# A hybrid encoder block on one core: the head in channel layout, a reordered SSM, and one gate chunk moved ahead of attention

## Chip, cores and metric

The kernel runs on one core of a Trainium2 chip. The metric is the device time of one execution in microseconds. All inputs are fp32, and a matmul operand is cut into two fp32r parts, a high part (a cast) and a low part (what the cast lost), so that one product costs three matmuls: high by high, high by low and low by high.

## What is computed

A block of 16 meta tokens and 1024 tokens (L = 1040) with 1024 channels passes through an RMSNorm, two mixers in parallel, a gated merge, an output projection, and then a convolutional FFN. Cut to what matters here:

```python
xn = rmsnorm(h, norm_mix_g)
q, k, v, f_logit, u, gates = split(xn @ w_in)
y_a = forgetting_attention(q, k, v, f_logit, b_forget) @ w_attn_out   # 8 heads of 64
z = gelu(s5(u, ...))                    # complex diagonal SSM, 32 groups of 16 channels, 64 states
zg = z @ w_glu
y_s = zg[..., :1024] * sigmoid(zg[..., 1024:])
g = sigmoid(gates)                      # 2048 wide
merged = g[..., :1024] * y_a + g[..., 1024:] * y_s
h = h + merged @ w_o
h = h + conv_ffn(rmsnorm(h, norm_ffn_g))
out = rmsnorm(h, norm_final_g)[16:]     # meta tokens dropped
```

## The kernel before

The program is written in one order, and a planner that simulates the run draws from it the order of instructions on each engine; on the chip each engine then keeps that order. `after(a, b)` pins `a` behind `b` on their engine without a semaphore. Tiles come from pools with a tag and a number of buffers; a tile waits until the last user of the buffer that it gets is done. Tags are shared between quite different tiles, so that, say, an x tile can sit in the place of an SSM table ("Gm", "Tm", "Wi", "sy", "tq").

**Head.** The normalised input is wanted with channels on partitions, as `xhi` and `xlo` [128, 8, 1040], for every projection from it. The first block of 272 tokens comes from the host already transposed (`x0t`): ScalarE casts it times g1 (L350), VectorE cuts the low part (L353), and the u product (`part`, L327 to L329) runs on features without the norm; the factor of each token, spread over the partitions through a transpose (L370), is multiplied in afterwards (L377). The other 768 tokens are loaded in rows, 128 a tile: a square with a running sum on ScalarE, a power on GpSimd, a multiply on VectorE (L340), eight transposes on TensorE (L191), a cast on ScalarE (L193) and a cut on VectorE (L129), and then the u product of their block (96 matmuls of 256 columns). Block 0's own normalised features are made last. u goes to memory (`u_d`) in 32 small stores and comes back grouped for the SSM.

**SSM.** `ssm` has three parts: small steps on VectorE on [128, 32] tiles, from the step sizes to the powers of lambda; a rotation table for either half of the groups; then for each quarter `tables(qt)`, with the output tables Gm and Tm (Tm through eight small transfers) and after them the input table Wi, and `chain(qt)`: U times Wi on TensorE, a rotation, two scans, a rotation back into the state St, and then Y = Gm St + Tm U, GELU, a store to `y_d`. The small steps may begin behind the features of tile 4.

**Gates.** `gate_chunk` makes 128 of the 2048 gate channels: 72 matmuls of 342 columns in three groups, each followed by a sigmoid and a store into `g_d`. The upper eight chunks are written after the SSM and fill TensorE beside it. Their weights come over GpSimd's queue and are cut by a cast and an accumulating transfer. The first chunk's weight (`gate0`) waits for the last features. The lower eight are spread between attention's steps, `GA = [2, 1, 1, 3]` for the four pairs of heads (the eighth follows attention), with a tanh in place of the sigmoid.

**Then** come `load_z` (32 small loads and the cuts of z and its sums), `forget_w` (the forget gate's weight), the first pair's q and k projection, `forget` (the forget gate, its log-sigmoid and running sum) and GLU in a seven-product block form.

Of the kernel before, what the change touches and what calls it, by code (L numbers as in the profile page):

```python
# [50 lines left out]
def block_kernel(ctx, tc, x, meta, g1, x0t, g1t, w_q, w_k, w_v, w_f, w_u, w_g, b_f, w_ao, lam_d, bw_d, cw_d,  # L51
# [118 lines left out]
    def norm_factor(pl, src, n, bufs=10, sq=None):  # L170
# [3 lines left out]
        S.activation(sq[:n], src, AF.Square, accum_out=ss[:n])  # L174
        va = pl.tile([P, 1], F, tag="vr", name="vr", bufs=3)
        V.tensor_scalar(va[:n], ss[:n], 1.0 / D, EPS, ALU.mult, ALU.add)
        rs = pl.tile([P, 1], F, tag="rs", name="rs", bufs=bufs)
        GP.tensor_tensor(rs[:n], va[:n], nhalf[:n], ALU.pow)
        return rs
# [107 lines left out]
    xa = [sp.tile([P, 4, UN], F, tag="tq", name="xa", bufs=3) for _ in range(2)]  # L287
    g1T = n1.tile([P, KD], F, name="g1T")
    S.dma_start(g1T, g1t)
    S.dma_start(xm, meta)  # L290
# [12 lines left out]
    xts = [sp.tile([P, D], F, tag=tag, name="xt", bufs=n) for tag, n in (("Wi", 2), ("Gm", 2), ("sy", 3)) for _ in range(n)]  # L303
    g1B = xts.pop(4)
    g1_load = S.dma_start(g1B, g1.partition_broadcast(P))

    place = dict(zip((3, 4, 1, 2, 5, 6), xts))
    place[0] = xm

    def load_x(i):  # L310
        load(place[i], x[P * (i - 1):P * i])

    for i in range(1, 7):
# [20 lines left out]
    def factors(i):  # L334
        n = TILES[i][1]
        return norm_factor(n1, place[i][:n], n)

    def features(i, rs, behind=None):
        t, n = TILES[i]
        xn = V.scalar_tensor_tensor(out=place[i][:n], in0=place[i][:n], scalar=rs[:n], in1=g1B[:n],  # L340
                                    op0=ALU.mult, op1=ALU.mult)
        if behind is not None:
            after(xn, behind)
        return to_feature(place[i], n, xhi, xlo, t)[-1]

    first = [mm_ps() for _ in range(4)]
    for j in range(4):
        for k in (2 * j, 2 * j + 1):
            src, hi = xa[j // 2][:, k % 4], xhi[:, k, :UN]
            cp_ = S.activation(hi, src, AF.Copy, scale=g1T[:, k:k + 1])  # L350
            if k == 1:
                after(g1_load, cp_)
            V.scalar_tensor_tensor(out=xlo[:, k, :UN], in0=src, scalar=g1T[:, k:k + 1], in1=hi.bitcast(F),  # L353
                                   op0=ALU.mult, op1=ALU.subtract)
        S.copy(uh[j], uraw[j])
        split_lo(V, ul[j], uraw[j], uh[j])
        for m in range(4):
            for k in (2 * j, 2 * j + 1):
                part(first[m], m, k, 0, UN)
    for i in (7, 8):  # L360
        place[i] = sp.tile([P, D], F, tag="Tm", name="xt", bufs=2)
        load_x(i)

    rs0 = [factors(i) for i in range(3)]
    tp = t_ps()
    for i, rs in enumerate(rs0):
        t, n = TILES[i]
        rb = sp.tile([P, P], F, tag="wi", name="rb", bufs=2)
        V.tensor_copy(rb[:n], rs[:n].broadcast_to([n, P]))
        PE.transpose(tp[:, t:t + n], rb[:n], ident[:n, :n])  # L370
    rsB = sp.tile([P, UN], F, tag="wr", name="rsB", bufs=2)
    S.copy(rsB, tp[:, :UN])
    for i in (3, 4):
        ready = features(i, factors(i))
    n_log = len(ssm_log)
    for m in range(4):
        V.tensor_tensor(us[m][:, :, :UN // CH], by_chunks(first[m][:, :UN]), by_chunks(rsB), ALU.mult)  # L377

    for b, (t, n) in enumerate(UBLK[1:]):
        if b:  # L380
            for i in (3 + 2 * b, 4 + 2 * b):
                last = features(i, factors(i))
        for m in range(4):
            ps = mm_ps()
            for k in range(KD):
                part(ps, m, k, t, n)
            S.copy(us[m][:, :, t // CH:(t + n) // CH], by_chunks(ps[:, :n]))
        if b == 2:
            for i in range(3):
                features(i, rs0[i], last)  # L390
# [4 lines left out]
    gate0 = [sp.tile([P, KD, P], dt, tag=tag, name="g0", bufs=n)  # L395
             for dt, tag, n in ((F, "Wi", 2), (R, "sy", 3), (R, "Wi", 2))]
    late.append(last)
    after(GP.dma_start(gate0[0], w_g[KD]), last)
    S.copy(gate0[1], gate0[0])
    lo_by_dma(gate0[2], gate0[1], w_g[KD])  # L400

# [4 lines left out]
    ssm_tables, ssm_chain = next(ssm_steps)  # L406
# [4 lines left out]
    def begin(q):  # L411
        ssm_tables(q)
# [3 lines left out]
    begin(0)  # L416
    begin(1)
    for q in range(4):
        run(chains[q])
# [5 lines left out]

    st_g = ExitStack()
    gp_ = pool(st_g, "gates", side="right")

    okeep = {}

    def gate_chunk(i, pl, tanh):
# [3 lines left out]
        for t, n in QBLK:  # L435
# [5 lines left out]
            else:  # L441
                gs = pl.tile([P, LQ // 3], F, tag="gs", name="gs", bufs=2)
                S.activation(gs, ps[:, :n], AF.Sigmoid)
                S.dma_start(g_d[P * i:P * i + P, t:t + n], gs)
# [7 lines left out]
    for i in range(KD, 2 * KD):  # L452
# [3 lines left out]
    st_f = ExitStack()  # L456
    fp = pool(st_f, "fgate", side="right")
    fraw = fp.tile([P, KD, H], F, name="fraw")
# [1378 lines left out]
```

## Time and profile before

| | us |
|---|---|
| three runs | 1481.59, 1489.31, 1491.31 |
| median of the runs | 1489.31 |
| span of the profiled execution | 1485.7 |
| TensorE busy in it | 1440.4 (97%) |
| VectorE, ScalarE, GpSimd busy | 1071.4, 712.2, 742.1 |

The profiled execution is one more execution; its own time is its span, from the first to the last instruction, and it lies inside the range of the three runs. PE is TensorE's matmuls and PEld its weight loads, DVE is VectorE, ACT ScalarE, POOL GpSimd, SP the engine that only issues transfers; L12 is line 12 of the kernel before. A matmul's own duration overlaps with the next one's, so that the pace is read from a stretch of time and a count and not from the mean of one; some matmul records can be missing. The granted clock is 1.00 where TensorE runs at full speed.

### The profile page before, as it was taken

What the parts mean: (1) busy time and instruction counts of PE and PEld (TensorE: products, weight loads), DVE (VectorE), ACT (ScalarE), POOL (GpSimd) and SP (SyncE); (2) the same over time, 40 slices, a digit from 0 to 9 for tenths busy, and PEclk for the clock granted to TensorE, in tenths of its full rate; (3) what the DMA queues carried; (4) which work ended last, traced back from release to release, by engine and by line L of the source; (5) the groups of instructions that cost most, each with busy time, mean ns of one, the idle gap of its engine ahead of it and who ended that gap; (6) DMA issues with size and microseconds to landing.
All of it is one profiled execution on the core that took longest, in us unless ns stands there. A gap on an engine that the chain in (4) does not pass through costs nothing. (4 is left out here: it accounts for less than half of the span.)

```text
span 1485.7 us, 26584 instructions
## 1 busy us (share of the span) xinstructions
PE 1440.4 (97%) x9712; PEld 1358.8 (91%) x9712; DVE 1071.4 (72%) x2173; ACT 712.2 (48%) x1384; POOL 742.1 (50%) x850
## 2 busy tenths in 40 slices
PE   7999997999999999999999999999999999998997
PEld 7989996998899999999888999999999999777886
DVE  6879648881566676647468987888877776788785
ACT  6434675541555665543546534444444445543433
POOL 1311125752456465524863144455544426789766
PEclk9999999999999999999999999999999999999999
DMA  6366571551127342047885135676653215765513
GB/s 246 86 157 157 128 163 50 177 160 43 48 79 178 93 111 90 26 148 256 257 158 185 57 109 141 178 199 188 174 143 100 84 57 180 286 203 148 168 40 114
DMA packets 91032, 206.72 MB, mean 139 GB/s; under 512 B 14651, under 2 KB 25531, under 8 KB 90517
## 3 DMA queue, kind: packets, MB, share of 16 engines
q1 hardware_dynamic: 69380, 159.73, 32.9%
q0 software_dynamic: 15296, 34.63, 13.2%
q10 hardware_dynamic: 6224, 10.65, 1.9%
q8 instruction: 77, 1.26, 0.3%
q14 instruction: 55, 0.44, 0.1%
HBM read 165.90 MB, written 69.35 MB: 158 GB/s over the span
## 5 line engine op out<-in xcount | busy, mean ns | idle before, releaser
L159 PE MATMUL mm<-xhi,whi 128*128 128x342 f32 (+2 forms) x488 | 159.4, 327 | 1.0 <-DVE q L129 1.0
L161 PE MATMUL mm<-xhi,wlo 128*128 128x342 f32 (+2 forms) x488 | 158.3, 325 | 0.0
L160 PE MATMUL mm<-xlo,whi 128*128 128x342 f32 (+2 forms) x488 | 157.7, 324 | 0.0
L1079 POOL TENSOR_TENSOR ov<-ov,og 128x1024 f32<-128x1024 f32 x21 | 51.1, 2434 | 125.6 <-ACT og L1078 121.7
L129 DVE TENSOR_TENSOR sw<-sf,sw 128x512 fp32r<-128x512 f32 x72 | 66.6, 925 | 50.0 <-ACT sw L1070 49.8
L1070 ACT CAST sw<-sf 128x512 fp32r<-128x512 f32 x72 | 44.9, 624 | 106.2 <-POOL sf L1196 74.5
L159 PEld LDWEIGHTS mm<-xhi,whi 128*128 128x128 f32 x488 | 91.9, 188 | 2.1 <-PE sp L714 0.8
L161 PEld LDWEIGHTS mm<-xhi,wlo 128*128 128x128 f32 x488 | 91.8, 188 | 0.3
L160 PEld LDWEIGHTS mm<-xlo,whi 128*128 128x128 f32 x488 | 91.9, 188 | 0.2
L763 ACT CAST th<-tp 128x256 fp32r<-128x256 f32 (+3 forms) x120 | 56.2, 472 | 62.5 <-PE tp L756 30.1
L129 DVE TENSOR_TENSOR tl<-tp,th 128x256 fp32r<-128x256 f32 (+3 forms) x120 | 65.2, 547 | 25.1 <-ACT th L763 23.7
L1196 POOL TENSOR_TENSOR sf<-raw,sf 128x512 f32<-128x512 f32 x36 | 59.1, 1641 | 44.8 <-DVE sw L129 44.7
L1196 POOL TENSOR_TENSOR sf<-raw 128x512 f32<-128x512 f32 x36 | 48.0, 1332 | 66.9 <-DMA raw<-in_w_up_dram 35.9
L221 PE MATMUL mm<-xhi,sw 128*128 128x258 f32 (+1 forms) x288 | 81.0, 281 | 0.0
L219 PE MATMUL mm<-xhi,sw 128*128 128x258 f32 (+1 forms) x288 | 80.8, 281 | 0.0
L220 PE MATMUL mm<-xlo,sw 128*128 128x258 f32 (+1 forms) x288 | 80.7, 280 | 0.0
L728 POOL TENSOR_SCALAR pt<-pt,nm 128x144 f32<-128x144 f32 (+4 forms) x72 | 51.8, 731 | 48.5 <-DVE nm L727 47.5
L1248 DVE SCALAR_TENSOR_TENSOR ov<-hv,cwt,ov 128x1024 f32<-128x1024 f32 x36 | 72.5, 2014 | 0.1
L1070 ACT CAST sw<-raw 128x512 fp32r<-128x512 f32 x70 | 43.0, 621 | 53.3 <-PE sp L221 25.5
L726 ACT ACTIVATE pt<-pt,nm 128x144 f32<-128x144 f32 (+4 forms) x72 | 52.9, 735 | 26.1 <-DVE nm L725 25.7
L719 DVE CUSTOM_DVE_ANT_0 pt<-sp,fb 128x328 f32<-128x328 f32 (+8 forms) x112 | 46.4, 430 | 20.0 <-PE sp L714 11.1
L756 PE MATMUL tp<-ident,pt 128*128 128x128 f32 (+1 forms) x360 | 58.3, 270 | 0.1
(708 smaller groups left out, 5702.1 us busy)
## 6 DMA issues: line engine op xcount, KB each, us to landing
raw<-in_w_up_dram SPq DMA_DIRECT2D x44, 512.0 KB, 3.6
t_d<-in_w_dn_dram POOLq DMA_DIRECT2D x44, 256.0 KB, 7.0
ar<-a_d SPq DMA_DIRECT2D x44, 256.0 KB, 5.1
wr<-t_d SPq DMA_DIRECT2D x44, 256.0 KB, 2.8
a_d<-ov SPq DMA_DIRECT2D x21, 512.0 KB, 2.6
wr<-in_w_dn_dram SPq DMA_DIRECT2D x33, 256.0 KB, 3.8
t_d<-in_w_dn_dram SPq DMA_DIRECT2D x22, 256.0 KB, 4.2
t_d<-t_d SPq DMA_DIRECT2D x22, 256.0 KB, 4.7
```

The source lines that it names most:

```text
L129: return eng.tensor_tensor(out_, src, hi.bitcast(F), ALU.subtract)
L159: yield PE.matmul(ps, whi[:, i, :], ahi[:, i], start=(i == 0), stop=False)
L160: yield PE.matmul(ps, whi[:, i, :], alo[:, i], start=False, stop=False)
L161: yield PE.matmul(ps, wlo[:, i, :], ahi[:, i], start=False, stop=(i == k - 1))
L219: PE.matmul(ps, a[0][:, i], bh, start=(i == 0 and not joins), stop=False, skip_group_check=True)
L220: PE.matmul(ps, a[0][:, i], bl, start=False, stop=False, skip_group_check=True)
L221: PE.matmul(ps, a[1][:, i], bh, start=False, stop=(i == kh - 1), skip_group_check=True)
L756: PE.transpose(tp[:kn, o:o + n], p_[:n, k0:k0 + kn], ident[:n, :n])
L763: S.copy(th[:kn, z:tw], tp[:kn, z:tw])
L1070: S.copy(hi, src)
L1196: sums.append(GP.tensor_tensor(f_, a, b, op))
L1248: V.scalar_tensor_tensor(out=o, in0=h_[:, j:SEQ + j], scalar=cwc(j, m), in1=o, op0=ALU.mult, op1=ALU.add)
```

## The change

- All 1040 tokens come transposed from the host (`xbt` for blocks 1 to 3), beside the row tiles that still give the factors. Blocks 0 and 1 go through the u product without the norm, and their u is multiplied by the factors later; blocks 2 and 3 are multiplied by the spread factors first. At the end blocks 0 and 1 get their normalised features in place. No x tile is transposed on the chip; the factors of all nine tiles are spread by a transpose.
- The first pieces of x and w_u are one channel block wide. meta, the step sizes and lambda come over GpSimd's queue; the broadcast of g1 is gone.
- The small steps may begin behind block 1's first features. The first gate chunk's weight is loaded without waiting for the last features, and the other gate weights wait for block 3's.
- `tables` is split into `input_tables` and `output_tables`. A quarter's input table and its U product come first; the output tables come after that quarter's state (for quarter 0 ahead of quarter 1's start). `dt8` is copied on ScalarE, and the second rotation is made in chain 2.
- y and the upper gate chunks go to memory over GpSimd's queue. Every second one of the eight loads of the last quarter of z goes there too.
- The forget gate's weight is made before the gate chunks and the gate itself straight after them, ahead of z and of the q/k projection.
- One chunk of the lower eight is made with the upper ones (`AHEAD = 1`), and attention's first pair has one less.

The diff, cut to its core:

```diff
-    for j in range(4):
-        load(xa[j // 2][:, 2 * (j % 2):2 * (j % 2) + 2], x0t[:, 2 * j:2 * j + 2])
-        load(uraw[j], w_u[:, 2 * j:2 * j + 2])
...
+    FIRST = [(0, 1), (1, 1), (2, 2), (4, 2), (6, 2)]
+    for k, n in FIRST:
+        load(xT[0][k // 4][:, k % 4:k % 4 + n], x0t[:, k:k + n])
+        load(uraw[k // 2][:, k % 2:k % 2 + n], w_u[:, k:k + n])
+
+    def load_block(b, tag):
+        xT[b] = [sp.tile([P, 4, UBLK[b][1]], F, tag=tag, name="xT", bufs=2) for _ in range(2)]
+        for h_ in range(2):
+            load(xT[b][h_], xbt[b - 1, :, 4 * h_:4 * h_ + 4])
...
+    load_block(1, "Wi")
+    for i in range(5, 9):
         load_x(i)
...
+    def factors(b):
+        tp = t_ps()
+        t0, n_ = UBLK[b]
+        for i in TB[b]:
+            t, n = TILES[i]
+            rs = norm_factor(n1, place[i][:n], n, behind=head[0])
+            rb = rbs[:n, i % 3]
+            V.tensor_copy(rb, rs[:n].broadcast_to([n, P]))
+            PE.transpose(tp[:, t - t0:t - t0 + n], rb, ident[:n, :n])
+        S.copy(spread[b], tp[:, :n_])
+
+    def features(b, k):
+        t, n = UBLK[b]
+        src, hi = xT[b][k // 4][:, k % 4], xhi[:, k, t:t + n]
+        cp_ = S.activation(hi, src, AF.Copy, scale=g1T[:, k:k + 1])
+        cut = V.scalar_tensor_tensor(out=xlo[:, k, t:t + n], in0=src, scalar=g1T[:, k:k + 1], in1=hi.bitcast(F),
+                                     op0=ALU.mult, op1=ALU.subtract)
+        return cp_, cut
+
+    def normed_features(b):
+        t, n = UBLK[b]
+        for q in range(2):
+            V.tensor_tensor(xT[b][q], xT[b][q], spread[b].unsqueeze(1).broadcast_to([P, 4, n]), ALU.mult)
+        return [features(b, k)[1] for k in range(KD)][-1]
...
+    load_block(2, "Tm")
+    load_block(3, "Gm")
+    for i in range(1, 5):
         load_x(i)
...
+    for b in (2, 3):
+        last = normed_features(b)
+        if b == 2:
+            gate0 = [sp.tile([P, KD, P], dt, tag=tag, name="g0", bufs=n)
+                     for dt, tag, n in ((F, "Tm", 2), (R, "sy", 3), (R, "Tm", 2))]
+            GP.dma_start(gate0[0], w_g[KD])
...
+        if b == 3:
+            for q in (0, 1):
+                factors(q)
+            for q in (0, 1):
+                normed_features(q)
         for m in range(4):
...
     def begin(q):
-        ssm_tables(q)
+        ssm_in(q)
         chains[q] = ssm_chain(q)
         next(chains[q])
 
     begin(0)
+    ssm_out(0)
     begin(1)
     for q in range(4):
+        next(chains[q])
+        if q:
+            ssm_out(q)
         run(chains[q])
...
-                S.dma_start(g_d[P * i:P * i + P, t:t + n], gs)
+                GP.dma_start(g_d[P * i:P * i + P, t:t + n], gs)
...
-    for i in range(KD, 2 * KD):
+    for i in [*range(KD, 2 * KD), *range(AHEAD)]:
         run(gate_chunk(i, gp_, False))
...
+    forget()
...
-                SY.dma_start(zt[GC * g:GC * g + GC], ym[g])
+                (GP if m == 3 and g % 2 else SY).dma_start(zt[GC * g:GC * g + GC], ym[g])
...
-    forget_w()
     qk = qk_tiles(0)
     run(project_qk(0, qk))
-    forget()
...
-    GA = [2, 1, 1, 3]
+    GA = [1, 1, 1, 3]
...
-            dt8 = big("dt8", [P, HQ, NCH])
-            V.tensor_copy(dt8, dec[:, qt * HQ:qt * HQ + HQ].unsqueeze(2).broadcast_to([P, HQ, NCH]))
...
+            S.copy(dt8, dec[:, qt * HQ:qt * HQ + HQ].unsqueeze(2).broadcast_to([P, HQ, NCH]))
+            GP.memset(dt8[:, :, 0:1], 0.0)
+            if qt == 2:
+                rot.append(rotation(1))
...
-            S.dma_start(y_d[qt], Y)
+            GP.dma_start(y_d[qt], Y)
```

More of the change, by code (lines that the diff above doesn't have):

```diff
@@ L347, in block_kernel @@
[L347 to L356, printed above, removed]
+    head = []
@@ new lines, in u_product, with us_part @@
+    def u_product(b, m):
+        ps = mm_ps()
+        for k in range(KD):
+            part(ps, m, k, *UBLK[b])
+        return ps
+    def us_part(b, m):
+        t, n = UBLK[b]
+        return us[m][:, :, t // CH:(t + n) // CH]
+    first = [mm_ps() for _ in range(4)]
+    for k0, n in FIRST:
+        j, sl = k0 // 2, slice(k0 % 2, k0 % 2 + n)
+        for k in range(k0, k0 + n):
+            features(0, k)
+        cp_ = S.copy(uh[j][:, sl], uraw[j][:, sl])
+        split_lo(V, ul[j][:, sl], uraw[j][:, sl], uh[j][:, sl])
@@ L357, in block_kernel @@
         for m in range(4):
[L358 removed]
+            for k in range(k0, k0 + n):
                 part(first[m], m, k, 0, UN)
[L360 to L361 removed]
+    head.append(cp_)
+    load_block(2, "Tm")
+    load_block(3, "Gm")
+    for i in range(1, 5):
         load_x(i)
[L364 to L374, printed above, removed]
+    for m in range(4):
+        S.copy(us_part(0, m), by_chunks(first[m][:, :UN]))
+    for k in range(KD):
+        ready = features(1, k)[1]
     n_log = len(ssm_log)
+    for b in (2, 3):
+        factors(b)
     for m in range(4):
[L377 to L382, printed above, removed]
-        for m in range(4):
[L384 to L390, printed above, removed]
+        ps = u_product(1, m)
+        S.copy(us_part(1, m), by_chunks(ps[:, :UBLK[1][1]]))
```

157 lines of the change are left out of this document (80 added, 77 removed).

## The prediction

> **What bounds the kernel now.** I read the page first, then the windows view cut at the points where the first 260 us change character, then TensorE's waits there.
>
> ```profile
> span 1485.7 us, 26584 instructions
> ...
> PE 1440.4 (97%) x9712; PEld 1358.8 (91%) x9712; DVE 1071.4 (72%) x2173; ACT 712.2 (48%) x1384; POOL 742.1 (50%) x850
> ```
>
> TensorE is busy for 97% of the span, so an edit can win only where TensorE stands idle, runs at a reduced clock, or has work taken from it. The windows view says where. Its columns are the busy time of each engine (instructions in brackets), then granted clock, DMA share and rate.
>
> ```profile
> core 0: us, PE busy (x) PEld busy (x) DVE busy (x) ACT busy (x) POOL busy (x), PEclk, DMA share, GB/s
> 0.00:7.30 7.30, 0.00 (x0) 0.00 (x0) 1.33 (x11) 3.30 (x5) 1.05 (x8) 1.00 0.71 198
> 7.30:23.00 15.70, 15.68 (x107) 15.35 (x107) 10.26 (x20) 12.01 (x21) 2.75 (x5) 1.00 1.03 412
> 23.00:26.20 3.20, 0.08 (x1) 0.00 (x0) 3.20 (x7) 3.17 (x7) 0.00 (x0) 0.88 0.92 365
> 26.20:33.00 6.80, 6.79 (x34) 6.57 (x35) 6.80 (x14) 4.07 (x8) 2.65 (x4) 0.55 0.03 9
> 33.00:73.50 40.50, 38.09 (x320) 37.04 (x319) 32.93 (x142) 15.12 (x30) 12.61 (x31) 1.00 0.30 75
> 73.50:98.00 24.50, 21.75 (x136) 20.86 (x137) 16.95 (x41) 7.28 (x15) 7.18 (x16) 0.93 0.89 214
> 98.00:195.20 97.20, 97.20 (x690) 95.37 (x688) 78.05 (x135) 52.25 (x90) 11.73 (x18) 1.00 0.56 136
> 195.20:224.80 29.60, 29.55 (x187) 29.23 (x185) 15.62 (x20) 22.62 (x33) 7.88 (x4) 1.00 0.65 141
> 224.80:238.00 13.20, 10.38 (x49) 8.66 (x49) 13.03 (x14) 7.01 (x17) 8.94 (x8) 0.74 0.15 41
> 238.00:257.00 19.00, 13.65 (x103) 12.40 (x102) 13.88 (x25) 11.05 (x21) 9.85 (x9) 1.00 0.11 30
> ...
> 390.00:455.00 65.00, 63.48 (x445) 61.79 (x446) 40.53 (x164) 36.06 (x84) 35.19 (x67) 1.00 0.18 57
> 455.00:640.00 185.00, 184.36 (x1288) 180.00 (x1287) 124.22 (x550) 108.82 (x265) 108.62 (x219) 1.00 0.39 104
> ```
>
> The head (u projection) runs to 73.5, SSM beside gate chunks to 195, the q/k projection to 225, the forget gate to 238, then GLU. Up to 257 TensorE is idle for 23.7 us by these rows: 7.3, 3.1, 2.4, 2.75, 2.8 and 5.35 us. Behind three of the gaps the clock is short: 0.55 over 6.8 us loses 3.05 us, 0.93 over 24.5 us loses 1.7, 0.74 over 13.2 us loses 3.4, of which I put some 0.8 inside the gap itself, so 2.6. The gaps have these causes:
>
> ```profile
> PE mm L327 <- ACT uh L355: 7.3, 1, 7.3
> PE sp L191 <- DVE vr L176: 3.1, 1, 3.1
> PE mm L518 <- POOL wf L129: 2.9, 1, 2.9
> PE sp L1730 <- ACT Wi L1714: 2.7, 1, 2.7
> ...
> PE sp L191 <- DVE xlo L129: 1.7, 1, 1.7
> ```
>
> They are the first weight cast, the transposes that wait for a normalised tile (twice), the forget weight, and SSM's input matrix, released late. The change touches every one of them. By the page "TensorE: Matmul & The Clock Gate" of the Trainium skill (part 1, the clock gate) the clock halves after an idle window of about 3.4 us, which would leave these gaps of 2.7 to 3.2 us unpunished and take 7 us off what the change can win; the rows with 0.55, 0.93 and 0.74 behind such gaps disagree, so that reading gets no weight here.
>
> **The change part by part.** *Head, TensorE.* Tokens of blocks 1 to 3 now arrive with channels on partitions, so the transposes of L191 go; nine transposes of a broadcast factor (three before) stay. A block of 96 matmuls keeps its pace:
>
> ```profile
> 44.00:55.44 11.44, 11.44 (x99) 11.44 (x98) 11.29 (x68) 2.16 (x6) 3.95 (x16) 1.00 0.00 0
> 124.00:134.10 10.10, 10.10 (x66) 9.93 (x65) 10.03 (x19) 7.06 (x9) 2.48 (x4) 1.00 0.69 200
> ```
>
> The first w_u piece holds one channel block instead of two, so the cast in front of the first matmul does half the elements and its transfer half the bytes: 7.3 becomes about 6.0 us. Block 0 keeps the 14.6 us from 7.3 to 21.9 that it has now, then three blocks of 11.44 us and about 1 us for the six added small transposes end at 6.0 + 14.6 + 34.3 + 1.0 = 55.9, against 73.5 now: 17.6 us at best. The pieces are the 3.1 and 2.4 us of gaps, 3.05 of clock, 1.3 at the start and some 7 of transposes. I keep 4 us for new waits of the same kind, since the factor transposes still sit in TensorE's order behind ACT's square and POOL's power: the gates start at 60, and the head wins 13.5 us (bounds 5, where one gap with its clock loss comes back and the gates wait for normalised blocks, and 17.6).
>
> *Head, DMA.* 768 tokens by 1024 channels, 3.1 MB of transposed x, are added and the 0.5 MB broadcast of g1 goes: at the 412 GB/s of the second row 6.4 us more traffic. x0t, w_u and block 1 are 4.3 MB, 10.3 us at that rate, so block 1 is there by 14 us and needed at 20.6; blocks 2 and 3, behind four x tiles, end at 8.5 MB, by 25 us, or by 30 with the waits for the tiles whose place they take, and are needed at 32 and 43.5. Cost on the path: 0. Without that cover each late 1 MB block would stop TensorE for 2.5 us.
>
> *Head, DVE and ACT.* These rows price the cut into high and low parts:
>
> ```profile
> L340 DVE SCALAR_TENSOR_TENSOR xt<-xt,rs 128x1024 f32<-128x1024 f32 x8 | 10.1, 1276 | 0.7 <-POOL rs L178 0.7
> L129 DVE TENSOR_TENSOR xlo<-tp,xhi 128x512 fp32r<-128x512 f32 x6 | 4.2, 698 | 0.0
> L353 DVE SCALAR_TENSOR_TENSOR xlo<-xa,g1T,xhi 128x272 fp32r<-128x272 f32 x8 | 3.6, 498 | 4.6 <-ACT xhi L350 4.6
> L350 ACT ACTIVATE xhi<-xa,g1T 128x272 fp32r<-128x272 f32 x8 | 3.7, 512 | 1.1 <-DMA xa<-in_x0t_dram 1.0
> ```
>
> Now two tiles cost DVE 2 x 1.28 + 4 x 0.69 = 5.3 us. A new block costs two 1024-wide multiplies at the 1.28 of L340 and eight cuts at no more than 0.5: 6.5 us. Over four blocks that is 4.8 us more, plus 4.0 for cutting block 1 a first time, so about 9 us more DVE work; ACT gets eight 0.51 us casts a block. DVE is busy for 54.5 of the first 73.5 us, so this fits before 73.5; but if the gates are to start at 56 it fills DVE completely, which is my second reason for the 4 us. So the SSM's small steps, though allowed earlier (behind block 1's cut, not behind tile 4), get their turn only in part earlier.
>
> *SSM.* Input tables and U's product go ahead of the output tables, dt8's copy goes to ACT, the second rotation moves behind chain 2's start. The work is nearly the same; what can go is DVE's idle time. To 195.2 the rows give DVE 149.5 us busy, so of the 190.6 us to its last SSM instruction, below, 41 are idle. With 9 us added and the idle time halved DVE is through by 179:
>
> ```profile
> 189.16 1.41 DVE L1456 TENSOR_TENSOR St<-ta,wr 64x516 f32<-64x516 f32 x2
> 205.71 0.89 DVE L129 TENSOR_TENSOR q<-mm,q 64x272 fp32r<-64x272 f32 x2 [15.13 <-ACT q L487]
> ...
> 240.27 0.70 DVE L129 TENSOR_TENSOR zlo<-zf,zhi 128x520 fp32r<-128x520 f32 x1
> ```
>
> From the last state at 190.6 to GLU's first matmuls at 238 pass 47 us (y out and in again, then DVE saturated with z's parts). The same 47 us from 179 give 226. If the last output table trails the last scan, its three 1.35 us products, a matmul set and the row transfers into Tm come on top, about 10 us: 236. I take 231.
>
> *Gate chunk and forget gate.* A chunk is 72 matmuls, at 10.10/66 = 0.153 us 11.0 us of TensorE, moved from attention to here. The forget weight is made ahead of the gates, so the 2.8 us gap and its 2.6 us of clock go. From 73.5 to 238 TensorE now needs 164.5 us, less 2.75 + 1.7 + 2.8 + 2.6 is 154.7, with the chunk 165.7: from 60 on GLU could start at 225.7, but z comes at 231. That is 5 us of new idle time and about 2 us of clock. Of GLU's 5.35 us of early gaps I keep 2.35, since the forget gate's scan and two table loads no longer fall among them. Attention's first pair then has the fill that pairs two and three have; the later pairs lose 0.64 us in 185, the first 1.5 in 65, so I charge 1 us (0 to 5, the upper end if the first pair's unequal chains set its pace).
>
> *Sum.* Point after GLU's first products: now 257. New: 231 + 2 + 13.65 + 2.35 = 249, less the 11.0 us that attention no longer does, plus 1: 239. That is 18 us; the 24 small stores' issues that leave ACT, in front of SSM's copies there, I value at 1 us more: 19 us. The profiled span of 1485.7 becomes 1466.7; the runs' median of 1489.3 lies 3.6 above the span, so I predict 1470.
>
> *Stores on POOL.* The gate chunks' stores move from ACT's queue to POOL's, a step that can cost.
>
> ```profile
> g_d<-gs ACTq DMA_DIRECT2D x24, 171.0 KB, 3.3
> u_d<-usb POOLq DMA_DIRECT2D x16, 65.0 KB, 7.7
> wlo<-in_w_g_dram POOLq DMA_DIRECT2D x2, 512.0 KB, 10.1
> 133.74 0.46 ACT L443 ACTIVATE gs<-mm 128x342 f32<-128x342 f32 x1 [2.72 <-DMA g_d<-gs]
> ```
>
> The page "DMA: Bandwidth & Descriptors" of the Trainium skill (SWDGE vs HWDGE vs iDMA) gives plain transfers to SP and ACT and keeps GpSimd for accumulating ones, so it speaks against this step; its fit for GpSimd's path would make one such store an estimated 2.4 us, and by that it would cost nothing. The POOL rows above are three to four times that under load. I charge 0 on the forecast, because a group of 24 matmuls takes 3.67 us, two buffers cover 7.3, and 7.7 + 0.46 is barely over that while SSM products stretch the groups.
>
> **The rivals.** *A: the head's time is given back at z.* If SSM ends no earlier, because DVE is full from the start, GLU starts at 238 as now. Then only the chunk (11.0) and 3 us of GLU's gaps are won, less 2 to 3 for clock and attention: 11 us, 1478. For: DVE's extra 9 us. Against: its 41 idle us. *B: every gap closes.* 17.6 in the head, 9.85 between 73.5 and 238, 4 in GLU: 31 us, 1458. For: each gap has its cure in the change. Against: the orders on the engines are fixed ahead, and the five rows of waits above are what such an order misses now. *C, slower: POOL's stores hold the gates.* A sigmoid waits for the store two groups earlier; each group then takes (0.46 + x)/2. With the 10.1 us of POOL's row that is 5.28 instead of 3.67, over 27 groups 43 us; four banks of PSUM let TensorE run 11 us ahead, and the forecast's 19 us come off: 13 us slower, 1503. It decides from x = 9.1 us on. For: one sigmoid already waits 2.72 us for a store that lands in 3.3, and ACT then holds up SSM's copies too. Against: the 10.1 falls in the crowded stretch, DMA share 0.89; behind it the share is 0.56.
>
> **How the numbers follow.** Forecast 0.45 (1462 to 1477), A 0.27, B 0.15, C 0.13. One per cent of 1489 is 15 us, about what a measurement of this kernel tells from no change; so faster is below 1474. That takes B and most of the forecast: 0.55; A, the forecast's upper edge and a trace of C are the same: 0.33; slower 0.12. The range starts below B's value by 4 us and ends inside C, 1454 to 1492.
>
> **What would show it.** Right: the first 128x342 gate matmul at 56 to 62; no transposes of x tiles in the head; no wait on wf and a clock of 1.00 in the forget gate; last St before 185; attention's first pair some 11 us shorter and no idler. Wrong: gates after 66 (head); GLU's first matmul after 236 with TensorE idle in front of it (A); POOL's g_d stores landing in over 9 us and ACT's sigmoids waiting for them (C); a first attention pair as long as before.

## The result, and the profile after

The changed kernel takes 1483.9 us (median of 20 runs, 1479.5 to 1488.0) where the kernel before took 1489.1 on the same chip (20 runs, 1481.6 to 1492.8). The ratio is 0.9971 with a 95% interval of [0.9959, 0.9982]: 4.3 us faster (1489.1 times 0.0029), where 19 were forecast. The profiled execution took 1486.4 us, 2.5 above its kernel's median, so differences of 2 or 3 us between the whole times of single traces are not read below.

The page of the changed kernel: TensorE is as full as before.

```profile
span 1484.7 us, 26535 instructions
...
PE 1440.5 (97%) x9646; PEld 1357.2 (91%) x9646; DVE 1079.2 (73%) x2197; ACT 725.6 (49%) x1420; POOL 759.0 (51%) x890
```

The windows of the changed kernel, columns as in the prediction's table: the end of the head, the gates with the SSM, the end of the SSM, the forget gate, the q/k projection, GLU's first products, and attention's first 128 us.

```profile
57.90:60.50 2.60, 0.23 (x2) 0.02 (x1) 2.60 (x3) 2.60 (x6) 1.96 (x5) 1.00 0.58 217
60.50:85.00 24.50, 24.46 (x145) 24.23 (x146) 24.45 (x79) 5.50 (x11) 14.59 (x27) 0.93 0.86 210
85.00:185.00 100.00, 98.42 (x690) 94.92 (x689) 83.35 (x141) 56.87 (x103) 24.40 (x42) 1.00 0.55 135
185.00:205.10 20.10, 16.60 (x105) 16.34 (x104) 0.00 (x0) 8.14 (x11) 3.07 (x5) 0.92 0.96 170
205.10:212.60 7.50, 7.50 (x50) 6.28 (x48) 1.64 (x2) 3.10 (x5) 4.97 (x7) 1.00 0.87 188
212.60:235.60 23.00, 23.00 (x146) 23.00 (x145) 19.26 (x20) 18.37 (x25) 3.27 (x4) 1.00 0.27 49
235.60:258.00 22.40, 15.96 (x99) 14.74 (x99) 21.36 (x37) 13.60 (x32) 14.20 (x13) 0.77 0.29 94
...
327.20:388.00 60.80, 58.58 (x274) 47.80 (x273) 19.45 (x47) 12.47 (x27) 19.09 (x32) 0.99 0.19 61
388.00:455.00 67.00, 65.73 (x434) 62.66 (x435) 44.26 (x198) 39.09 (x95) 36.69 (x79) 0.94 0.16 51
```

TensorE's longest waits from 55 to 400 us (engine, tile and line that waited, what ended the wait; us in total, times, longest):

```profile
PE tp L1813 <- DMA raw<-in_w_glu_dram: 3.5, 1, 3.5
PE sp L223 <- DVE ops L129: 2.5, 1, 2.5
PE mm L159 <- ACT xhi L366: 2.4, 1, 2.4
PE sp L748 <- DVE nm L762: 2.1, 1, 2.1
PE mm L221 <- ACT ops L616: 2.0, 1, 2.0
PE tp L1813 <- DMA Tm<-Kt: 1.5, 1, 1.5
```

And three marks of each kernel by the view of one line, where the last two times are the starts of the first and the last instruction of the group: the SSM's last state on VectorE, its last Y product, and attention's scores. First the kernel before, then the changed one.

```profile
L1456 DVE TENSOR_TENSOR St<-ta,wr x8: 690/692/693, 117.4 to 189.9; 64x516 f32<-64x516 f32 x8
L1770 PE MATMUL tp<-St,Gm x32: 272/275/275, 121.8 to 194.9; 128*128 128x130 f32 x32
L713 PE MATMUL sp<-k,q x120: 171/323/457, 325.7 to 641.5; 128*128 128x264 f32 x16, 128*128 128x328 f32 x16, 128*128 128x392 f32 x16, 128*128 128x456 f32 x16
```

```profile
L1491 DVE TENSOR_TENSOR St<-ta,wr x8: 690/692/694, 112.4 to 183.8; 64x516 f32<-64x516 f32 x8
L1811 PE MATMUL tp<-St,Gm x32: 272/275/422, 115.4 to 199.1; 128*128 128x130 f32 x32
L748 PE MATMUL sp<-k,q x120: 170/324/702, 327.2 to 637.8; 128*128 128x264 f32 x16, 128*128 128x328 f32 x16, 128*128 128x392 f32 x16, 128*128 128x456 f32 x16
```

The accounts of the two traces, stage by stage:

| stage | before | after | won |
|---|---|---|---|
| to the first gate matmul | 73.5 | 60.5 | 13.0 |
| from there to GLU (238.0; 235.6) | 164.5 | 175.1 | -10.6 |
| GLU, to attention's first scores (325.7; 327.2) | 87.7 | 91.6 | -3.9 |
| first to last scores | 315.8 | 310.6 | 5.2 |
| behind the last scores | 844.2 | 846.9 | -2.7 |

The rows add up to the 1.0 us between the two spans. The last row is a part whose code the change leaves as it was: 1.7 us of it are one stretch of half clock at 1366 us, behind a wait of 2.95 us that fell almost whole into one window of the clock (TensorE busy for 0.65 of 3.41 us), where the same wait before, 3.01 us, was split over two windows (2.08 and 1.72 us busy) and cost no clock; the last section has more on this.

The head wins its 13 us. The second row should have cost 1.2 us: the moved chunk's 11.0 less the 9.85 of stalls and lost clock that stood there before. It costs 10.6, because 8.4 us of new stalls took the place of the old ones: 1.7 of clock in 60.5 to 85, behind a gap ahead of the gates, 1.6 idle in 85 to 185, and 3.5 idle with 1.6 of clock in 185 to 205, where TensorE's Y products wait for Tm; about 1 us is left that these rows do not name. (The wait of 3.5 us is put down to a load of GLU's weight; it is L1813, the product with Tm, that stands, and the transfers into Tm left just ahead of that load on SP's queue.) In GLU's first 22.4 us TensorE is idle for 6.4 and at 0.77 of its clock, 5.2 more: 11.6 us. That sum counts the half clock in idle time too: in the 10.24 us at half clock TensorE was busy for 6.62 (the row below), so that some 9.8 us were lost, where 5.35 were before. The sums of idle time and clock in the experiments are upper bounds in the same way. And attention wins 5.2 us of the chunk's 11.0; one wait of 2.1 us for the first maxima has a long stretch of low clock behind it.

```profile
239.55:249.79 10.24, 6.62 (x27) 6.05 (x28) 10.01 (x16) 6.87 (x16) 8.54 (x7) 0.50 0.43 131
```

The last state starts 6.1 us earlier than before, yet the last Y product starts 4.2 us later. VectorE's timeline around it, and what its engine was last waiting for:

```profile
183.12 1.42 DVE L1491 TENSOR_TENSOR St<-ta,wr 64x516 f32<-64x516 f32 x2
210.96 0.49 DVE L515 SCALAR_TENSOR_TENSOR fl__2416<-po,bf,fx 8x272 f32<-8x272 f32 x1 [26.42 <-ACT fx L514]
211.37 1.91 DVE L596 TENSOR_TENSOR zf<-zt 128x520 f32<-128x520 f32 x1
```

VectorE stands for 26.4 us there, and stood once before for 8.6 us ahead of a Gm, with no instruction named that released it (its waits from 60 to 185 us):

```profile
DVE Gm L1491 <- issue: 8.6, 1, 8.6
```

That Gm is the last quarter's and starts at 145.83 us, when the last Y product that reads quarter 1's Gm (145.39 to 145.78) has just ended. Gm has two buffers, so by these times VectorE stood there for the buffer.

In the long stretch, first in its order is the forget gate's add (L515), which needs the forget gate's matmuls on TensorE (205 us); z's sums (L596) stand behind it. From 211 on it has everything at once, z's parts, the forget gate, the cuts of q and k and of GLU's weights, and is full until 254: the 21.36 of 22.40 in GLU's first window.

### The profile page after: what moved, and what is told of

The parts are those of the page before. It is cut to its first block, busy times and chain, and to the rows that moved or that the text cites. A ratio compares the mean times of both kernels' runs of the same rounds, so it can differ in the third digit from the quotient of the medians.

```text
span 1484.7 us, 26535 instructions
## 1 busy us (share of the span) xinstructions
PE 1440.5 (97%) x9646; PEld 1357.2 (91%) x9646; DVE 1079.2 (73%) x2197; ACT 725.6 (49%) x1420; POOL 759.0 (51%) x890
## 5 line engine op out<-in xcount | busy, mean ns | idle before, releaser
L129 DVE TENSOR_TENSOR sw<-sf,sw 128x512 fp32r<-128x512 f32 x72 | 70.3, 977 | 51.6 <-ACT sw L1105 51.3
L129 DVE TENSOR_TENSOR sw<-raw,sw 128x512 fp32r<-128x512 f32 x70 | 56.0, 803 | 5.5 <-ACT sw L1105 4.9
```

The source lines that it names most:

```text
L129: return eng.tensor_tensor(out_, src, hi.bitcast(F), ALU.subtract)
```

## The experiments

Each was timed beside the kernel before on its own chip, so ratios are compared and not medians. "Won" is 1489.1 us times (1 - ratio).

| kernel | ratio to before | won, us |
|---|---|---|
| the change | 0.9971 [0.9959, 0.9982] | 4.3 |
| 1 last output table early | 0.9958 [0.9942, 0.9974] | 6.3 |
| 2 forget gate behind q/k | 0.9982 [0.9969, 0.9995] | 2.7 |
| 3 chunk back in attention | 0.9952 [0.9934, 0.9969] | 7.1 |
| 4 stores on ScalarE | 0.9966 [0.9952, 0.9981] | 5.1 |
| 5 more lead in attention | 0.9950 [0.9934, 0.9965] | 7.4 |
| 6 chunk from the last pair | 0.9959 [0.9943, 0.9974] | 6.1 |
| 7 = 1 and 2 | 0.9927 [0.9911, 0.9942] | 10.9 |
| 8 = 1, 2 and 5 | 0.9912 [0.9899, 0.9925] | 13.1 |
| 9 the head alone | 0.9940 [0.9926, 0.9953] | 8.9 |
| 10 output tables early | 0.9945 [0.9933, 0.9958] | 8.2 |
| 11 first gates from the end | 1.0033 [1.0021, 1.0045] | -4.9 |
| 12 = 8 and 11 | 0.9922 [0.9909, 0.9936] | 11.6 |
| 13 = 10 and 2 | 0.9919 [0.9902, 0.9937] | 12.1 |
| 14 = 10, 2 and 5 | 0.9897 [0.9883, 0.9912] | 15.3 |

The intervals of runs 1 to 6 overlap with the change's own, so these are read by their traces; 7 to 10 and 12 to 14 lie clear of it on the fast side, 11 on the slow side.

**1. The last output table ahead of quarter 2's products.**

```diff
-        if q:
-            ssm_out(q)
+        for k in ((), (1,), (2, 3), ())[q]:
+            ssm_out(k)
```

> The changed kernel, with the output tables of the SSM's last quarter written ahead of the products of quarter 2 instead of behind the last scan. Theory T1 (the stretch from the gates to GLU is set by z: the last output table trails the last scan, its eight transfers land at 193.8 us, the last Y product ends at 199.4 us, and VectorE, with z's parts behind the forget gate, is late for GLU): the last Y product ends by 193, and of the 6.4 us of idle time and 5.1 us of lost clock in 235.6 to 258 at least half goes; 4 to 7 us faster than the changed kernel. Theory T2 (the time is lost because the moved gate chunk leaves attention's first pair without enough work for TensorE, idle time and a half clock between 327 and 400 us): nothing moves behind 327 us, less than 2 us in all. Theory T3 (GpSimd's stores are the brake): less than 2 us.

The view of the Y products, VectorE's waits and the window of GLU's first 23 us:

```profile
L1811 PE MATMUL tp<-St,Gm x32: 272/275/378, 115.7 to 187.8; 128*128 128x130 f32 x32
```

```profile
DVE zf L596 <- DMA zt<-y_d: 11.9, 1, 11.9
DVE fl__2416 L515 <- ACT fx L514: 10.0, 1, 10.0
```

```profile
229.00:252.00 23.00, 17.32 (x111) 16.30 (x110) 21.34 (x37) 14.43 (x33) 14.68 (x13) 0.78 0.29 92
```

Half of T1 is shown: the last Y product starts 11.3 us earlier (187.8), and GLU 6.5 us earlier (229.1). The other half is not: GLU's first 23 us still lose 5.7 us to idle time and 5.1 to the clock. The loss moves along with GLU, since VectorE still waits for z's loads and then for the forget gate, and is then full again (21.34 of 23.00).

**2. The forget gate behind the q/k projection**, as before the change, with its two tiles in GLU's buffers again.

```diff
-    forget()
...
     run(project_qk(0, qk))
+    forget()
```

> The changed kernel, with the forget gate put back behind the first q/k projection; its weight stays early. T1 in its second half (VectorE stands idle for 26 us, 184.5 to 211, because the forget gate's first step is ahead of z's parts in its order, and is then full until 254): VectorE's idle stretch shrinks to under 15 us, z's parts end before 245 instead of 254, and GLU's first 22 us lose less than 5 us to idle time and clock instead of 11.5; 3 to 7 us faster than the changed kernel. If the idle stretch is only y's way to memory and back, the stretch stays and the time stays within 2 us. T2 and T3: within 2 us.

```profile
DVE q L129 <- ACT q L544: 21.9, 1, 21.9
```

```profile
235.10:258.00 22.90, 19.46 (x140) 18.48 (x141) 16.35 (x28) 12.95 (x25) 12.12 (x13) 0.93 0.18 55
```

GLU's first window now loses 5.0 us instead of 11.6 (3.4 idle, 1.6 of clock), as expected of T1, yet the time did not fall: the forget gate itself, now between q/k and GLU, leaves TensorE idle for 2.3 us, and VectorE's idle stretch only changed its name, because y is late either way. This cure has nothing to free as long as the Y products end at 196 us.

**3. The chunk back in attention.**

```diff
-    AHEAD = 1
+    AHEAD = 0
...
-    GA = [1, 1, 1, 3]
+    GA = [2, 1, 1, 3]
```

> The changed kernel, with the gate chunk back in attention's first pair (none of the lower eight ahead). T2: the 2.2 us of idle time and the 5.1 us of clock in attention's first pair go, TensorE's work is the same, and nothing else moves: 5 to 7 us faster than the changed kernel. T1: TensorE now reaches GLU's place at 224.6 us, 11 us earlier, but z does not, so that 8 to 11 us of new idle time stand ahead of or inside GLU's first products, against the 5 to 7 us won in attention: 2 to 6 us slower. T3: within 2 us.

```profile
DVE fl__2325 L515 <- ACT fx L514: 15.1, 3, 9.1
```

```profile
222.70:245.00 22.30, 13.95 (x73) 12.07 (x72) 21.71 (x29) 12.63 (x27) 15.50 (x10) 0.77 0.23 71
```

T1 expected this slower and it is not: 2.8 us faster by the ratios, with overlapping intervals. TensorE came to GLU 12.9 us earlier, and the loss in GLU's first 22 us grew only from 11.6 to 13.5 us (8.4 idle, 5.1 of clock). So z is no wall at a fixed time, as I had it: with a chunk less, the forget gate's matmuls begin at 186 instead of 205 (the last of them at 199, behind the Y products), VectorE gets past them earlier, and its full stretch moves with them. Attention's side came out as T2 said: 315.9 us from first to last scores as before, with no clock lost.

**4. The stores back on ScalarE's queue.**

```diff
-                GP.dma_start(g_d[P * i:P * i + P, t:t + n], gs)
+                S.dma_start(g_d[P * i:P * i + P, t:t + n], gs)
...
-            GP.dma_start(y_d[qt], Y)
+            S.dma_start(y_d[qt], Y)
```

> The changed kernel, with the stores of y and of the upper gate chunks back on ScalarE's queue. T3 (GpSimd's stores cost): the landing falls below the 2 to 4.3 us of the changed kernel and it gets 3 us faster or more. T1 and T2: the stores are beside the path, so only ScalarE's 27 x 3 added issues of some 0.05 us count, in front of the SSM's copies: 0 to 2 us slower.

The stores' row of the transfers (queue, count, size, median us from issue to landing), first of the changed kernel, then of this one:

```profile
g_d<-gs POOLq DMA_DIRECT2D x26, 171.0 KB, 4.3
```

```profile
g_d<-gs ACTq DMA_DIRECT2D x27, 171.0 KB, 3.2
```

The landing gets 1.1 us shorter and the time moves by 0.8 us, inside both intervals: T3 has no support. The expectation's 0.05 us for an issue and its count were wrong: 27 issues in all, of 0.33 us each (median 326 ns) on ScalarE's queue, and even so nothing shows in the time.

**5. More matmuls of lead in attention's first pair.**

```diff
-            for _ in range(24):
+            for _ in range(48):
```

> The changed kernel, with 48 instead of 24 matmuls of the next pair's projection run ahead of attention's first pair, so that fewer are left for its steps. Theory T2a (attention wins 5 us instead of 11 because, with a chunk less, the first score groups have only 0.5 us less of other matmuls between them, and one wait of 2.1 us for the first maxima, at 384 us, puts the clock at half for 10.2 us behind it): the wait falls under 0.7 us, the clock is 1.00 in 388 to 455, and from GLU's end to the end of attention's scores pass 305 to 307 us instead of 311; 4 to 6 us faster than the changed kernel. T2b (a pair needs the whole chunk as filler everywhere): the idle time moves to later steps of the pair, within 2 us. T1 (the losses lie ahead of GLU alone): within 2 us.

```profile
L748 PE MATMUL sp<-k,q x120: 171/324/457, 328.2 to 633.3; 128*128 128x264 f32 x16, 128*128 128x328 f32 x16, 128*128 128x392 f32 x16, 128*128 128x456 f32 x16
```

T2a is shown: from first to last scores pass 305.1 us, 10.7 less than before the change, so attention keeps all of the chunk but 0.3 us. The slowest score product falls from 702 to 457 ns, that is, none runs at half clock any more, and the wait at 384 us is gone. The time is 3.1 us better by the ratios, at the edge of the interval. The other traces bear it out: in all eight with one chunk less in the first pair and 24 matmuls of lead (the change and runs 1, 2, 4, 7, 10, 11 and 13) the clock is at half for 6.8 or 10.2 us between 375 and 401 us, and in none of the eight others.

**6. The chunk taken from the last pair instead.**

```diff
-    GA = [1, 1, 1, 3]
+    GA = [2, 1, 1, 2]
```

> The changed kernel, with attention's first pair back at two gate chunks and its last pair at two instead of three. T2a (it is the place of the lost chunk that matters, the first score groups): no wait at 384 us, the last pair has 144 matmuls of filler for 28 places, 5 a place where pairs two and three have 7 to 10, and stays busy but for 1 to 2 us: 3 to 6 us faster than the changed kernel. T2b (a chunk is filler wherever it is): the last pair idles for 4 to 8 us more and the clock there falls below 0.95: within 2 us of the changed kernel, or slower.

From first to last scores it took 307.1 us (325.7 to 632.8): 3.5 us of the lost 5.8 come back, without a wait at 384 us. That is 2.0 us more than in run 5, but not idle time: TensorE idles for 3.2 us there against 2.9, and 12 more matmuls stand between the first and the last scores (1988 against 1976). It is the place of the missing chunk that matters (T2a), and the time, 0.9959, cannot be told from the change's.

**7. Runs 1 and 2 together.**

> The changed kernel, with both edits of the first and the second run: the last output table ahead of quarter 2's products, and the forget gate behind the first q/k projection. T1 as it stands now (with the table alone VectorE waits 11.9 us for z's loads and 10.0 us for the forget gate's matmuls, and is full behind them; with the forget gate alone it waits 21.9 us for q because y is late): the last Y product ends by 190, VectorE has z's parts done before the q/k projection ends, GLU's first 23 us lose under 4 us to idle time and clock instead of 11: 7 to 10 us faster than the changed kernel, 3 to 5 us faster than the run with the table alone. If VectorE's sheer amount of work ahead of GLU (z's parts, the forget gate, the cuts of q and k and of GLU's weights) is the bound: GLU's first 23 us lose 7 us or more as before, and the gain is that of the table alone, 2 to 7 us.

```profile
229.20:252.20 23.00, 18.17 (x141) 17.11 (x141) 16.09 (x28) 13.87 (x28) 12.73 (x13) 1.00 0.20 58
```

6.6 us better than the change and 4.6 better than run 1, nearly as T1 expected. GLU starts at 229.2, its first window loses 4.8 us and no clock, and VectorE is busy for 16.1 of its 23 us instead of being full. Each cure had needed the other: the early table brings y, the late forget gate leaves VectorE free for it.

**8. Runs 1, 2 and 5 together.**

> The same, and 48 instead of 24 matmuls run ahead of attention's first pair. If T1 and T2a hold, the gains add: 11 to 16 us faster than the changed kernel, 1468 to 1473 us. If only one holds: 4 to 9 us faster.

```profile
199.04 1.22 DVE L593 TENSOR_TENSOR zf<-zt 128x520 f32<-128x520 f32 x1 [13.37 <-DMA zt<-y_d]
```

8.8 us better than the change, less than the sum expected of both. Attention took 304.9 us as in run 5. What went missing lies ahead of it: GLU started at 235.3 instead of the 229.2 of run 7, which has the same order on TensorE and VectorE up to attention, because z's first sum came 3.7 us later in this execution (199.0 against 195.4 us, each behind z's loads); TensorE then waited 2.4 us for a cut of q on VectorE, with 1.7 us of clock behind it. A profile is one draw; the ratios differ by 2.2 us in favour of this kernel.

**9. The head alone**: the output tables right behind each quarter's start, forget gate behind q/k, no chunk ahead, stores on ScalarE (the edits of runs 2, 3, 4 and 10). The split tables with the input table first, dt8's copy on ScalarE, the second rotation in chain 2, the early forget weight and z's loads on GpSimd's queue stay in it, so that the head is alone against the four undone steps and not against every other one.

> The head of the changed kernel, with all later steps as before: output tables right behind each quarter's start, forget gate behind the q/k projection (its weight stays early), the gate chunk back in attention, stores of y and gates on ScalarE's queue. Theory T1 (what the head wins is given back at z, because the SSM does not end as much earlier): gates start at 60 instead of 73.5, GLU starts within 5 us of 225 because TensorE has 11 us less to do ahead of it, but its first 23 us lose 8 us or more to idle time and clock; from GLU's end on as before; 1481 to 1485 us, 4 to 8 us faster than before. Rival T4 (the losses of the changed kernel come from its other steps, and the head alone keeps its 13 us): GLU's first 23 us lose no more than the 5.4 us of before, 1474 to 1478 us.

```profile
L1490 DVE TENSOR_TENSOR St<-ta,wr x8: 690/692/694, 112.6 to 177.6; 64x516 f32<-64x516 f32 x8
L1810 PE MATMUL tp<-St,Gm x32: 273/275/379, 117.3 to 182.9; 128*128 128x130 f32 x32
```

```profile
211.30:227.70 16.40, 10.57 (x50) 7.42 (x49) 16.19 (x18) 12.34 (x25) 11.10 (x6) 0.79 0.00 0
227.70:250.70 23.00, 20.51 (x139) 19.64 (x140) 17.75 (x31) 14.10 (x29) 11.91 (x13) 0.85 0.23 71
```

The rows are the forget gate and GLU's first 23 us. This is the run that turned the account over. The head alone wins 8.9 us, more than the whole change, and near T4: the four undone steps together cost 4.6 us, although one of them moves 11 us of work out of attention. And the head's 13 us do reach the SSM's end: the last state comes at 177.6 and the last Y product at 182.9, each 12 us earlier than before. So what T1 took for granted, that the SSM cannot follow the head, is wrong; what is given back (in the forget gate 5.8 us idle and 3.4 of clock, in GLU's first 23 us 2.5 and 3.4) lies behind the SSM.

**10. The output tables right behind each quarter's start**, in the changed kernel otherwise.

```diff
     begin(1)
+    ssm_out(1)
     for q in range(4):
         next(chains[q])
-        if q:
-            ssm_out(q)
         run(chains[q])
         if q < 2:
             begin(q + 2)
+            ssm_out(q + 2)
```

> The changed kernel, with each quarter's output tables right behind its start again, so that no output table trails a scan; the forget gate, the chunk and the stores stay as changed. T1: the last Y product ends 6 to 9 us earlier than 199.4, as in the first run, if the earlier tables do not push the scans back by as much; 2 to 5 us faster than the changed kernel. If putting the input tables first is what lets the scans end early, the last state comes 4 us or more later on VectorE and the time stays within 2 us of the changed kernel.

```profile
L1491 DVE TENSOR_TENSOR St<-ta,wr x8: 691/693/694, 109.8 to 177.2; 64x516 f32<-64x516 f32 x8
L1811 PE MATMUL tp<-St,Gm x32: 272/275/378, 112.6 to 182.7; 128*128 128x130 f32 x32
```

With the tables in their place the last state comes 6.6 us earlier than in the changed kernel, not later, and the last Y product 16.4 us earlier. Putting them behind the state gained nothing and cost both. The time is 3.9 us better.

**11. The first gate chunk's groups from the last tokens to the first.**

```diff
-        for t, n in QBLK:
+        for t, n in (QBLK[::-1] if i == KD else QBLK):
```

> The changed kernel, with the three groups of the first gate chunk made from the last tokens to the first, so that the ready blocks 2 and 3 come first. Theory T5 (the wait of 2.4 us at 57.9 us, and the half clock of 3.4 us behind it, come from the gates' first group reading blocks 0 and 1, the last to be normalised): the wait goes, the clock in 62 to 85 rises from 0.93 to 1.00, TensorE gets 4 us ahead; the time itself moves by 0 to 2 us, because z, not TensorE, sets GLU's start (T1). If TensorE set it, 4 us faster than the changed kernel.

```profile
PE mm L160 <- DVE xlo L367: 2.4, 1, 2.4
```

```profile
237.70:260.70 23.00, 14.24 (x75) 12.84 (x74) 21.82 (x30) 11.92 (x30) 11.97 (x11) 0.70 0.23 68
```

A miss. The gates start at 57.8 instead of 60.5, but the same 2.4 us are waited a few matmuls later, for the low part of the features, and the half clock follows there too: the wait was for normalising blocks 0 and 1 as such, not for the order of reading them. The run is 9.2 us slower than the change; GLU's first 23 us lose 15.7 (8.8 idle, 6.9 of clock), and the last state comes 2.8 us later. Why VectorE's order became so much worse, I did not settle. **12**, all cures with this one, gives nothing over run 8 (0.9922 against 0.9912):

> The changed kernel with four edits: last output table ahead of quarter 2's products, forget gate behind the q/k projection, 48 matmuls of lead in attention's first pair, and the first gate chunk's groups from the last tokens to the first. T1, T2a and T5 together: with z no longer late TensorE's 4 us ahead of the SSM count in part; 0 to 4 us faster than the run with the first three, 1471 to 1475 us. If GLU's start is set by VectorE all the same: no gain over that run.

**13 and 14. The changed kernel with the output tables and the forget gate put back, the chunk kept (edits of runs 10 and 2); then also with run 5's edit.**

> The changed kernel with two of its steps undone and the others kept: output tables right behind each quarter's start, forget gate behind the q/k projection; the chunk ahead of attention and GpSimd's stores stay. Theory T1 as the runs have shaped it (the head's 13 us reach Y, 183 instead of 195 us, as long as no output table trails; then z's parts have VectorE to themselves as long as the forget gate stands behind the q/k projection): TensorE, with the chunk, comes to GLU at 232 to 236 us, z is there, GLU's first 23 us lose under 4 us; attention wins 5 us by the chunk; 1473 to 1476 us, 3 to 5 us faster than the head alone. Rival T6 (the moved chunk is neutral or costs, whatever stands around it: what it takes from attention it puts ahead of GLU, where VectorE is the limit): GLU at 238 us or later, 1477 to 1481 us, no faster than the head alone.

> The same with 48 instead of 24 matmuls of lead in attention's first pair. T1 and T2a: attention wins the whole chunk, 11 us; 1468 to 1473 us, 3 to 5 us faster than the run beside it. T6: 1475 to 1479 us.

Attention's scores of either:

```profile
L747 PE MATMUL sp<-k,q x120: 170/324/702, 317.5 to 626.8; 128*128 128x264 f32 x16, 128*128 128x328 f32 x16, 128*128 128x392 f32 x16, 128*128 128x456 f32 x16
```

```profile
L747 PE MATMUL sp<-k,q x120: 171/323/457, 320.8 to 626.0; 128*128 128x264 f32 x16, 128*128 128x328 f32 x16, 128*128 128x392 f32 x16, 128*128 128x456 f32 x16
```

With the two late steps undone run 13 wins 12.1 us, 3.2 more than the head alone. Its median, 1476.4, lies between the two ranges, and its interval overlaps with run 9's: by itself it leans to T1 (the chunk pays once z is early; GLU starts at 230.5 us and its first 23 us idle for 4.4 at full clock) and no more. With the lead the chunk is won in whole, 305.2 us in attention, and run 14 wins 15.3 us, clear of run 9: T6 is out. (Run 9 with the lead alone was not made. But its attention takes 316.2 us at full clock, with 3.2 us idle in all, so the lead could not have won the 6.4 us between the two there.) Its median, 1474.0, is the lowest seen, 11 us better than the change by the ratios, and one above what was expected.

## Why the prediction was wrong, step by step

In the traces the forecast's span is missed by 18.0 us (1466.7; 1484.7). Of these 4.6 are GLU's start (231; 235.6), 4.9 are GLU's own stage (86.7 by the sum; 91.6), 4.8 attention (305.8 by the sum; 310.6) and 2.7 the part behind it; the last 1.0 is what the stores were to free on ScalarE, which no stage shows.

**Head: right.** Gates at 60.5 where 60 was said, 13.0 us won where 13.5 was said; no transposes of x tiles, no late block, and of the 4 us kept back for new waits one of 2.4 us took most, with 1.7 us of clock behind it in the next stage.

**SSM: the size was right for another order.** "DVE through by 179" came out at 184.5. With the output tables right behind each quarter's start (runs 9 and 10) it is 178, in run 10 with 155.8 us busy and 22.1 idle, where the forecast had 158.5 and 20.5: the estimate of VectorE's work and idle time holds, and the step that it left out is the reordering itself, whose last output table, and an idle stretch of 8.6 us ahead of a Gm in VectorE's order, cost 6 us.

**The step that failed: "I take 231".** The text had the other case in it, an output table that trails the last scan, and priced it at 10 us, GLU at 236. It happened (235.6), and I took the middle instead of reading the order of the diff, in which `ssm_out(q)` stands behind `next(chains[q])` for the last quarter too. What the runs showed in its place: the trailing table moves the last Y product by 16 us, and GLU by the 5 us between the two (with the tables early it starts at 230.8, run 10).

**The second: "Of GLU's 5.35 us of early gaps I keep 2.35", since the forget gate is out of them.** They became some 9.8 us with their clock. The forget gate left TensorE's way and got into VectorE's: in front of z's parts, where VectorE waited 26.4 us for it (shown by run 7 against run 1, 4.6 us). I named POOL's and SP's queues as places where a moved step can hold others up, and not VectorE's.

**The third: all stalls from 73.5 to 238 go.** The wait and the clock at the forget gate did go (row 205.10: no idle time, clock 1.00). In their place stand the 8.4 us of new ones in the account above, 6.7 of them behind 85 us, where I had counted the SSM's waits as cured. So 225.7 was not in reach for this order.

**The chunk: charged 1 us, cost 5.8.** The bound was 5, "if the first pair's unequal chains set its pace"; it was nearly that, one gap of 2.1 us and 10.24 us of half clock behind it. Run 5 moved 24 matmuls and won 10.7 of 11.0, so the 1 us was right but for that gap.

**Stores on POOL: right**, 4.3 us to landing where rival C decided from 9.1, and nothing won by taking them back (run 4).

**Rivals.** A ended nearest (1478), but by another way: SSM did end earlier, and could have ended earlier still. B's price is not reached either; run 14, with every step in a good place, lies 4 us above the forecast. With its two late steps undone the change comes to attention when the prediction said: at 317.5 in run 13, where the sum gives 325.7 - (257 - 249) = 317.7 (run 14's single trace came there at 320.8).

## What to carry to other kernels

A step moved out of one engine's way stands in another's order: before costing a move at nothing, list what is queued behind its instructions on every engine, the vector engine first, and what they wait for. Time won early is kept only if the last producer of the next stage, not the first, moves with it; look in the diff at what is issued for the last tile. And a chunk of filler is worth its length only if the places that it leaves, above all the first one after a change of stage, are filled from elsewhere.

## What the runs showed of the hardware

The clock's half steps lie on a grid. In the 16 traces there are 74 stretches of half clock; in each trace their beginnings are whole multiples of 3.413 us apart, and they last one, two, three or four times that (the last of a run aside); where the grid lies differs from one execution to the next. Cut on its grid (without the last 20 us of each trace, shares to the nearest per cent), a window at full clock in which TensorE had no matmul for 55% or more was followed by half clock in 53 of 53 cases, one idle for 20 to 54% in 5 of 165. Two grid windows of the changed kernel with what follows the first, and two of run 3:

```profile
58.65:62.06 3.41, 1.52 (x9) 1.52 (x10) 3.41 (x5) 3.41 (x9) 2.03 (x5) 1.00 0.87 315
62.06:65.47 3.41, 3.41 (x14) 3.41 (x13) 3.41 (x7) 1.23 (x4) 3.12 (x6) 0.50 1.06 192
382.94:386.35 3.41, 1.19 (x9) 0.72 (x6) 1.51 (x15) 2.08 (x5) 2.07 (x9) 1.00 0.00 0
```

```profile
190.65:194.06 3.41, 2.01 (x12) 1.28 (x10) 0.98 (x2) 0.47 (x1) 0.00 (x0) 1.00 0.86 161
194.06:197.48 3.42, 2.25 (x20) 2.29 (x21) 0.00 (x0) 0.48 (x1) 0.00 (x0) 1.00 1.11 232
```

The gap of 2.1 us at 384.3 lies in one window (1.19 of 3.41 busy) and was followed by three at half clock; the 2.6 us that run 3 idled in a row were split between two windows (2.01 and 2.25 busy) and cost no clock. So a gap of 2 to 3 us is a draw, at 1.7 us a window, and some of the spread between runs of one kernel, and between single traces here, is that draw. Why the clock stayed at half for three windows behind 386, with TensorE busy in all of them, the runs don't show. By the page "TensorE: Matmul & The Clock Gate" of the Trainium skill (part 1, the clock gate) the window is about 3.4 us long and runs free of the kernel. The traces agree with that to the figure (3.413 us). The same page of the Trainium skill has the clock at half after at least one idle window. Read as a window without any matmul, the traces do not bear that out: 55% of one was enough, and the prediction was right to give that reading no weight.
